# Two experts' weights side by side in one transfer, and the router's low parts on VectorE

## The chip, the cores and the metric

The kernel runs on one core of a Trainium2 chip. A core has TensorE (PE in the profile), VectorE (DVE), ScalarE (ACT), GpSimd (POOL), the queue engine SyncE (SP, which issues nearly all loads here), 16 DMA engines, and two on-chip memories: SBUF, 128 partitions wide, and PSUM, which TensorE writes. The metric is the device time of one execution in microseconds (us); lower is better.

## The reference, cut to what matters

The program is two dense transformer layers followed by two layers of a second kind. Each layer of the second kind is a sequence mixer, a layer norm, and a mixture of experts with 32 experts for 256 tokens of 1024 features. Only the mixture of experts is touched:

```python
def hierarchical_moe(x, w_rg, b_rg, w_re, b_re, w_gate, w_up, w_down):
    g_prob = softmax(xt @ w_rg + b_rg)                 # 4 groups
    g_w, g_idx = top_k(g_prob, 1)
    e_logits = (xt @ w_re + b_re).reshape(n_tok, 4, 8) # 8 experts in each group
    e_logits = take_along_axis(e_logits, g_idx)
    e_w, e_local = top_k(softmax(e_logits), 2)
    gate = g_w * e_w / sum(e_w)
    # each token goes through its two experts:
    h = silu(x @ w_gate[e]) * (x @ w_up[e])            # 1024 -> 512
    y += gate * (h @ w_down[e])                        # 512 -> 1024
# and around it: h = layer_norm(ALPHA * h + ffn)
```

An expert has three float32 matrices of 2 MB each (1 MB is 1,048,576 bytes here). All 32 experts of both layers are read, 192 MB a layer.

## The kernel before, in words

The function `moe` is called once for each of the two layers. It has three stretches.

**Loads.** The weights come in pieces of 1 MB, one piece for one half (`q`) of one matrix of one expert, 128 partitions of 8 KB. Their order is fixed in the list `order`: experts go in pairs, and stage by stage it holds gate and up of pair `st` and down of pair `st - 1`. They go through 20 places of 1 MB (`EW`): 3 in the tile `ew0`, 6 in `ew1`, 4 in `w` (the mixer's own weight ring), 5 in `hx` (the mixer's tile `hl`, where a piece is cut into two loads of 512 KB, 128 partitions of 4 KB), and one each in `x` and `xw`. `prefetch` (lines 1549 to 1559) issues loads on SP in that order; a load waits until TensorE has finished with what the place held before. The places come free at the end of the mixer one after another, the last two (`x`, `xw`) when the router has chosen.

**Router** (lines 1570 to 1664). For two tiles of 128 tokens: the normed rows `hc` on VectorE, 16 transposes and the logits on TensorE, then a chain of small VectorE instructions that finds the group and the two experts (`first_max`), ending in the choice matrix `M` (L1658). Three small matmuls on it give every token its place (`pos`, L1664). TensorE works in a mode whose operands are split into a high part `hH` (written by ScalarE, L1605) and a low part `hL = hc - hH` (written by GpSimd, L1606). The residual `ALPHA * h` is started in the accumulators by matmuls over `hH`, again `hH`, and `hL` (L1617).

**Experts** (lines 1752 to 1835). For every two pairs `gather` compares positions (`sel`, L1679) and multiplies `hH` and `hL` by the result (L1693), which gathers 64 tokens for each of 4 experts into `XG`. `first_products` (L1769) multiplies gate and up: the two experts of a pair fill the two halves of the array's columns, and the order of `steps` takes them in turn. Only in gate of the first pair are the steps sorted, all of one expert and then all of the other. `gated`, `turned`, `second_products` (L1797) and `combine` (L1809) follow. TensorE's order there is the order of the code (`manual_schedule`); elsewhere a scheduler sets it.

The two lines that the prediction speaks of most:

```python
for kk, i in sorted(steps, key=lambda s: s[1]) if (pr, nm) == (0, "gate") else steps:   # 1766
nc.gpsimd.tensor_tensor(hL[:, t], hc[:, t], hH[:, t].bitcast(F32), op=OP.subtract)       # 1606
```

Of the kernel before, what the change touches and what calls it, by code (L numbers as in the profile page):

```python
# [18 lines left out]
P = 128  # L19
S = 256  # L20
# [1475 lines left out]
EW = (("ew0", 3), ("ew1", 6), ("w", 4), ("hx", 5), ("x", 1), ("xw", 1))  # L1496
NX = sum(n for _, n in EW)


def moe(k, l, h, hsum, rows, const, cc):  # L1500
# [5 lines left out]

    names = [n for n, slots in EW for _ in range(slots)]
    for n, slots in EW:
        if n[:2] == "ew":
            k.rings[n] = (0, k.t(W, [P, slots, 2048], n))  # L1510
        elif n[0] == "x":
            k.rings.pop(n, None)
    k.rings["hx"] = (0, k.t(k.const, [P, 10, 1024], "hl", F32, 1))
    nsl, later = [0], []

    def wtile(src, ab, now):
        n = nsl[0]
        nsl[0] += 1
        ring = names[n % NX]
        if ring != "hx":  # L1520
            if ring not in k.rings:

                k.rings[ring] = (0, k.t(k.const, [P, 1, 2048], ring))
                k.late(k.rings[ring][1], anchor=M[:, 1, :1])
            w = k.slot(ring)
            wv = w.rearrange("p (a b) -> p a b", a=ab)
            if n < NX and ring[:2] == "ew":
                k.late(w, anchor=k.early)
            nc.sync.dma_start(wv[:, :now], src[:, :now])
            if now < ab:  # L1530
                later.append((wv[:, now:], src[:, now:]))
            return lambda i: wv[:, i]
        hs = []
        for q in range(2):
            w = k.slot("hx")
            wv = w.rearrange("p (a b) -> p a b", a=ab // 2)
            nc.sync.dma_start(wv, src[:, q * ab // 2:(q + 1) * ab // 2])
            hs.append(wv)
        return lambda i: hs[i // (ab // 2)][:, i % (ab // 2)]


    order = [((nm, q, e), a["moe_" + nm][l, e, q], 4)
             for st in range(NE // 2 + 1) for nm, pr in (("gate", st), ("up", st), ("down", st - 1))
             if 0 <= pr < NE // 2 for q in range(2) for e in (2 * pr, 2 * pr + 1)]
    index = {key: n for n, (key, _, _) in enumerate(order)}
    tiles = {}
    nxt = [0]

    def prefetch(n):
        while nxt[0] < min(n, len(order)):  # L1550
            key, src, ab = order[nxt[0]]
            tiles[key] = wtile(src, ab, ab // 2 if nxt[0] >= len(order) - 2 else ab)
            nxt[0] += 1
        if n >= len(order):

            while later:
                nc.sync.dma_start(*later.pop(0))
# [16 lines left out]
    for t in range(NT):  # L1574
# [3 lines left out]
        nc.vector.scalar_tensor_tensor(hc[:, t], h[:, t], mean, rows[0], op0=OP.add, op1=OP.mult)  # L1578
# [16 lines left out]
    nc.vector.tensor_tensor(boff, p, br, op=OP.add)  # L1595
    gl, el = k.t(W, [P, NT, 4], "rt"), k.t(W, [P, NT, NE], "rt2")
    for t in range(NT):
        for dst, cs in ((el, slice(4, 36)), (gl, slice(0, 4))):
            nc.vector.scalar_tensor_tensor(dst[:, t], plg[:, t, cs], ms[t][:, 2:3], boff[:, cs], op0=OP.mult, op1=OP.add)
    for t in range(NT):  # L1600
        for q in range(2):
            sl = slice(512 * q, 512 * q + 512)
            nc.vector.scalar_tensor_tensor(hc[:, t, sl], hc[:, t, sl], ms[t][:, 2:3], rows[1][:, sl],
                                           op0=OP.mult, op1=OP.add)
        nc.scalar.activation(hH[:, t], hc[:, t], AF.Copy)  # L1605
        nc.gpsimd.tensor_tensor(hL[:, t], hc[:, t], hH[:, t].bitcast(F32), op=OP.subtract)  # L1606
# [51 lines left out]
    nc.vector.tensor_tensor(v(M), v(M), og4, op=OP.mult)  # L1658
# [5 lines left out]
    nc.vector.scalar_tensor_tensor(pos, p, 1.0, M, op0=OP.add, op1=OP.mult)  # L1664
# [4 lines left out]
    slots = k.t(A, [P, 4, S], "slots", F32R)  # L1669

    def gather(pr, after=None):
# [42 lines left out]
    at = {}  # L1714
# [265 lines left out]
```

## Time and profile before

| | us |
|---|---|
| median of 3 timed runs | 1922.09 (1921.82 to 1927.83) |
| the profiled execution's own time | 1928.14 |
| its span in the profile | 1926.5 |
| mean granted TensorE clock, as a share of 2.4 GHz | 0.975 |

The page cuts the span into 40 slices. Two plateaus stand out in its row of gigabytes per second, slices 18 to 25 and 32 to 39: these are the two layers' expert stretches. TensorE is busy 94% of the span, but matmuls are pipelined and a busy TensorE may still be one that waits for its input, so the plateaus of the load row and the waits have to be read together.

### The profile page before, as it was taken

The page shows a single profiled execution, that of the slowest core. Times are in us where ns is not written, and L with a number is a line of the kernel's source. Part 1 is how long each engine was busy: PE and PEld are TensorE (multiplying, and loading weights), DVE is VectorE, ACT ScalarE, POOL GpSimd, SP SyncE. Part 2 cuts the span into 40 slices and gives each one's busy share as a digit, 9 for nine tenths or more (in the row PEclk, how much of TensorE's full clock was granted, in tenths as well). Part 3 has the DMA queues.
Part 4 walks back from the last instruction along what each step waited for, and adds up shares of the span by engine and source line. Part 5 has one row for each costly group of instructions (what it writes and reads, how often), then busy time and mean ns, then how long its engine had stood idle before and what let it go on. Part 6 is the DMA issues. An engine that isn't in the chain of part 4 may idle for free. (4 is left out here: it accounts for less than half of the span.)

```text
span 1926.5 us, 30281 instructions
## 1 busy us (share of the span) xinstructions
PE 1811.1 (94%) x12598; PEld 1231.2 (64%) x12598; DVE 770.3 (40%) x1491; ACT 595.2 (31%) x1022; POOL 134.7 (7%) x267
## 2 busy tenths in 40 slices
PE   8999999999998899999999999889999999999896
PEld 7889998989998788644444343377984444443333
DVE  5754545655456978411111011067782111111012
ACT  5554444554445644211111011144441111111011
POOL 1100000010010411100000000012120000000000
PEclk9999999999999999799999999998998999999998
DMA  6345554245563327799999999841488999999995
GB/s 250 109 153 196 177 204 154 88 146 183 194 224 132 112 89 312 264 414 418 418 418 418 418 418 418 358 168 46 143 332 328 413 418 418 418 418 418 418 418 206
DMA packets 90307, 541.65 MB, mean 281 GB/s; under 512 B 10416, under 2 KB 10928, under 8 KB 37936
## 3 DMA queue, kind: packets, MB, share of 16 engines
q1 hardware_dynamic: 87552, 531.21, 70.1%
q0 software_dynamic: 2320, 8.24, 1.4%
q8 instruction: 103, 1.69, 0.4%
q14 instruction: 44, 0.36, 0.1%
q10 hardware_dynamic: 288, 0.15, 0.0%
HBM read 538.52 MB, written 1.05 MB: 280 GB/s over the span
## 5 line engine op out<-in xcount | busy, mean ns | idle before, releaser
L161 DVE TENSOR_TENSOR hl<-w,hl 128x1024 fp32r<-128x1024 f32 (+2 forms) x252 | 295.6, 1182 | 224.3 <-ACT hl L159 218.2
L159 ACT ACTIVATE hl<-w 128x1024 fp32r<-128x1024 f32 (+2 forms) x252 | 256.4, 1026 | 282.2 <-PE aux L129 103.0
L1769 PE MATMUL aux<-ew_e,XG_e 128*64 128x512 f32 x992 | 253.9, 595 | 8.5 <-DMA ew_e<-in_moe_up 8.5
L1779 DVE SCALAR_TENSOR_TENSOR e_sh_e<-e_sh_e,e_kept_e,aux 128x512 f32<-128x512 f32 x32 | 23.9, 747 | 509.7 <-ACT e_sh_e L1778 497.0
L1769 PEld LDWEIGHTS aux<-ew_e,XG_e 128*64 128x64 f32 x992 | 82.2, 137 | 166.2 <-issue 148.1
L1788 ACT ACTIVATE e_sh_e<-m 128x512 f32<-128x512 f32 x32 | 19.1, 598 | 509.2 <-PE m L1786 509.2
L1769 PE MATMUL aux<-hl,XG_e 128*64 128x512 f32 x480 | 137.4, 604 | 10.1 <-DMA hl<-in_moe_up 6.1
L129 PE MATMUL aux<-hl_f,hl 128*128 128x256 f32 x1056 | 131.1, 283 | 0.6 <-DVE hl_f L245 0.3
L129 PEld LDWEIGHTS aux<-hl_f,hl 128*128 128x128 f32 x1056 | 129.3, 191 | 2.8 <-DVE hl_f L245 0.7
L1769 PE MATMUL aux<-w,XG_e 128*64 128x512 f32 x384 | 126.6, 594 | 4.5 <-DMA w<-in_moe_gate 4.5
L1801 DVE TENSOR_TENSOR e_y_e<-m,e_y_e 128x512 fp32r<-128x512 f32 x64 | 44.2, 691 | 215.0 <-ACT e_y_e L1800 215.0
L129 PE MATMUL m<-hl_f,hl 128*128 128x256 f32 x1056 | 129.7, 283 | 0.0
L129 PEld LDWEIGHTS m<-hl_f,hl 128*128 128x128 f32 x1056 | 127.7, 191 | 0.0
L182 PE MATMUL mm<-hl,m_f 128*128 128x512 f32 x528 | 123.4, 390 | 0.0
L1797 PE MATMUL m<-ew_e,e_sh_e 128*64 128x512 f32 x448 | 117.3, 602 | 0.0
L182 PEld LDWEIGHTS mm<-hl,m_f 128*128 128x128 f32 x528 | 97.8, 188 | 19.4
L1800 ACT ACTIVATE e_y_e<-m 128x512 fp32r<-128x512 f32 x64 | 38.2, 597 | 201.5 <-PE m L1797 201.5
L1769 PEld LDWEIGHTS aux<-hl,XG_e 128*64 128x64 f32 x480 | 41.8, 138 | 81.9 <-issue 51.6
L1693 PE MATMUL m<-e_y_e,e_h_e 128*128 128x256 f32 x256 | 69.2, 308 | 24.2 <-DVE e_y_e L1679 24.2
L1809 PE MATMUL mm<-e_y_e,slots_e 128*128 128x512 f32 x256 | 78.3, 429 | 6.1 <-PEq L1832 4.8
L1797 PE MATMUL m<-w,e_sh_e 128*64 128x512 f32 x240 | 81.5, 606 | 0.0
L1797 PEld LDWEIGHTS m<-ew_e,e_sh_e 128*64 128x64 f32 x448 | 35.6, 138 | 68.0 <-issue 63.6
(571 smaller groups left out, 2710.7 us busy)
## 6 DMA issues: line engine op xcount, KB each, us to landing
ew_e<-in_moe_gate SPq DMA_DIRECT2D x62, 1024.0 KB, 16.2
ew_e<-in_moe_up SPq DMA_DIRECT2D x62, 1024.0 KB, 17.4
ew_e<-in_moe_down SPq DMA_DIRECT2D x56, 1024.0 KB, 18.6
w<-in_w_gate_up SPq DMA_DIRECT2D x44, 1024.0 KB, 4.9
w<-in_w_in SPq DMA_DIRECT2D x36, 1024.0 KB, 5.0
hl<-in_moe_up SPq DMA_DIRECT2D x60, 512.0 KB, 11.4
hl<-in_moe_down SPq DMA_DIRECT2D x60, 512.0 KB, 13.2
hl<-in_moe_gate SPq DMA_DIRECT2D x60, 512.0 KB, 13.3
```

The lines of the kernel that those rows point to most:

```text
L129: self.nc.tensor.matmul(out, x, y, start=(i == 0 and j == 0), stop=(i == n - 1 and j == len(terms) - 1))
L159: nc.scalar.activation(vo(hv), s, AF.Copy)
L161: nc.vector.tensor_tensor(vo(lv), s, vo(hv).bitcast(F32), op=OP.subtract)
L182: self.nc.tensor.matmul(acc[t][h], u1, u2, start=(kg == 0 and q == 0), stop=(kg == n_k - 1 and q == len(terms) - 1))
L1693: nc.tensor.matmul(p[:, j], src[:, t, c], sel[t], start=n == 0, stop=n == 3)
L1769: nc.tensor.matmul(p[64 * i:64 * i + 64], xg[:, 4 * q + kk, o:o + CAP], tiles[nm, q, e](kk), start=(q == 0 and kk == 0), stop=(q == 1 and ...
L1779: i = nc.vector.scalar_tensor_tensor(s_, s_, at[pr][1], up, op0=OP.mult, op1=OP.mult)
L1788: nc.scalar.activation(hh, p, AF.Copy)
L1797: nc.tensor.matmul(p[64 * i:64 * i + 64], hh[:, f, 64 * i:64 * i + 64], tiles["down", hf, es[i]](f), start=f == 0, stop=f == 3)
L1800: nc.scalar.activation(yh, p, AF.Copy)
L1801: nc.vector.tensor_tensor(yl, p, yh.bitcast(F32), op=OP.subtract)
L1809: nc.tensor.matmul(acc[t][hf], sT[:, t * P:(t + 1) * P], ys[:, 2 * hf + q], start=False, stop=pr == last and q == 1)
```

## The change

What was two loads for two experts becomes one of 2 MB. The arrays in memory are laid out anew (`pack3`), so that the same partition's rows of both experts of a pair lie side by side: 16 KB in one run. The 20 places of 1 MB become 10 of 2 MB in the same tiles and of the same total. Two of the ten are made of two separate 1 MB places (`ew0` with `hx`, and `x` with `xw`) and still take two loads of 8 KB rows; the places in `hx` no longer take loads of 4 KB rows. The sorted order in the first gate is gone. The low parts `hL` are computed by VectorE, tile 0 after `M`, tile 1 after `sel`; their residual matmuls stand where the first, empty `combine` was, the gather takes both `hH` before both `hL`, and several router instructions get an `issue_after` that fixes their order. The small tile `al` lies in `slots` now.

```diff
-EW = (("ew0", 3), ("ew1", 6), ("w", 4), ("hx", 5), ("x", 1), ("xw", 1))
-NX = sum(n for _, n in EW)
+EW = (("ew0", 3), ("ew1", 6))
+NX, SPLIT = 10, 6
...
+    places = [("ew0", 0), ("ew1", 0), ("ew1", 2), ("ew1", 4), ("w", 2 * turn), ("w", 2 - 2 * turn),
+              (("ew0", 2), ("hx", 4)), ("hx", 0), ("hx", 2), (("x", 0), ("xw", 0))]
...
+    def fetch(n, parts=(0, 1)):
+        nm, q, pr = order[n]
+        src, at_ = a["moe_" + nm][l, pr, q], places[n % NX]
+        if type(at_[0]) is str:
+            t = part(*at_, 2)
+            if n < NX and at_[0][0] == "e":
+                k.late(t, anchor=k.early)
+            t = four(t)
+            now = 2 if n == len(order) - 1 else 4
+            nc.sync.dma_start(t[:, :, :now], src[:, :, :now])
...
+        for i in parts:
+            t = part(*at_[i], 1)
...
+            nc.sync.dma_start(t, src[:, i:i + 1])
...
-        nc.vector.scalar_tensor_tensor(hc[:, t], h[:, t], mean, rows[0], op0=OP.add, op1=OP.mult)
+        last = nc.vector.scalar_tensor_tensor(hc[:, t], h[:, t], mean, rows[0], op0=OP.add, op1=OP.mult).ins
...
-        nc.gpsimd.tensor_tensor(hL[:, t], hc[:, t], hH[:, t].bitcast(F32), op=OP.subtract)
...
+    def low_parts(t, after):
+        with tc.issue_after(after):
+            return nc.vector.tensor_tensor(hL[:, t], hc[:, t], hH[:, t].bitcast(F32), op=OP.subtract).ins
...
-    for src, i in ((hH, 0), (hH, 1), (hL, 0)):
+    def residual(src, i):
         for t in range(NT):
             for hf in range(2):
                 nc.tensor.matmul(acc[t][hf], al[:, i], src[:, t, hf * 512:(hf + 1) * 512],
                                  start=src is hH and i == 0, stop=False)
+    residual(hH, 0)
+    residual(hH, 1)
...
-    nc.vector.tensor_tensor(v(M), v(M), og4, op=OP.mult)
+    last = low_parts(0, nc.vector.tensor_tensor(v(M), v(M), og4, op=OP.mult).ins)
...
+        if pr == 0:
+            tail.append(low_parts(1, placed))
...
-                for t in range(NT):
-                    for src in (hH, hL):
+                for src in (hH, hL):
+                    for t in range(NT):
                         nc.tensor.matmul(p[:, j], src[:, t, c], sel[t], start=n == 0, stop=n == 3)
...
-                for kk, i in sorted(steps, key=lambda s: s[1]) if (pr, nm) == (0, "gate") else steps:
-                    e = es[i]
-                    o = (e % 4) * CAP
-                    nc.tensor.matmul(p[64 * i:64 * i + 64], xg[:, 4 * q + kk, o:o + CAP], tiles[nm, q, e](kk),
+                for kk, i in steps:
+                    o = (es[i] % 4) * CAP
+                    nc.tensor.matmul(p[64 * i:64 * i + 64], xg[:, 4 * q + kk, o:o + CAP], tiles[nm, q, pr](i, kk),
...
     def combine(pr, hf):
+        if pr == -1 and hf == 1:
+            residual(hL, 0)
...
-        o["moe_" + n] = i[f"moe_w_{n}_2"].reshape(L, NE, 2, 4, P, 512).swapaxes(3, 4)
+        o["moe_" + n] = i[f"moe_w_{n}_2"].reshape(L, NE // 2, 2, 2, 4, P, 512).transpose(0, 1, 3, 5, 2, 4, 6)
```

Three places show how the built programs differ. First SP, in the first of the two layers, from the mixer's last output weights on to the first loads that reuse a place. `128x2048` is a load of 1 MB, `128x1024` one of 512 KB, `128x4096` one of 2 MB. Before:

```order
L144 DMA w_67<-in_w_out 128x2048
L1529 DMA ew_e_704_7682<-in_moe_gate 128x2048 x2
L1529 DMA ew_e_705_7683<-in_moe_gate 128x2048
L1529 DMA ew_e_705_7683<-in_moe_up 128x2048 x4
L1529 DMA ew_e_705_7683<-in_moe_gate 128x2048
L1529 DMA w_67<-in_moe_gate 128x2048 x3
L1529 DMA w_67<-in_moe_up 128x2048
L1537 DMA hl_7684<-in_moe_up 128x1024 x6
L1537 DMA hl_7684<-in_moe_down 128x1024 x3
L1529 DMA x_7920<-in_moe_down 128x2048
L1537 DMA hl_7684<-in_moe_down 128x1024
L1529 DMA xw_7923<-in_moe_down 128x2048
```

And in the changed program:

```order
L144 DMA w_67<-in_w_out 128x2048
L1544 DMA ew_e_705_7683<-in_moe_gate 128x4096
L1544 DMA ew_e_705_7683<-in_moe_up 128x4096 x2
L1554 DMA ew_e_704_7682<-in_moe_up 128x2048
L1544 DMA w_67<-in_moe_gate 128x4096 x2
L1554 DMA hl_7684<-in_moe_up 128x2048
L1544 DMA hl_7684<-in_moe_up 128x4096
L1544 DMA hl_7684<-in_moe_down 128x4096
L1554 DMA x_7898<-in_moe_down 128x2048
L1554 DMA xw_7901<-in_moe_down 128x2048
```

The order of the bytes is the same; a load into `w` now needs two of the ring's four slots, and no `hl` load stands behind `x`. Second TensorE in the router, around the last logits (`aux`, with the transposed rows `hT`) and the residual matmuls (`mm_7814` and so on are accumulators, `e_h` and `e_l` are `hH` and `hL`). Before:

```order
L1584 MATMUL mm_7774<-const_69,XG_e_711_7725 128x128
L1617 MATMUL mm_7814<-e_h_e_709_7723,mw_e_729_7810 128x512
L1617 MATMUL mm_7815<-e_h_e_709_7723,mw_e_729_7810 128x512
L1617 MATMUL mm_7814<-e_h_e_709_7723,mw_e_729_7810 128x512
L1588 MATMUL aux_7728<-e_misc_e_707_7717,hT_e_724_7779 128x36 x4
L1617 MATMUL mm_7815<-e_h_e_709_7723,mw_e_729_7810 128x512
L1617 MATMUL mm_7814<-e_l_e_710_7724,mw_e_729_7810 128x512
L1617 MATMUL mm_7815<-e_l_e_710_7724,mw_e_729_7810 128x512
```

And in the changed program:

```order
L1593 MATMUL mm_7757<-const_69,XG_e_711_7708 128x128 x4
L1597 MATMUL aux_7711<-e_misc_e_707_7700,hT_e_722_7751 128x36 x4
L1597 MATMUL aux_7711<-e_misc_e_707_7700,hT_e_724_7762 128x36 x4
L1635 MATMUL mm_7795<-e_h_e_709_7706,slots_e_729_7791 128x512
L1635 MATMUL mm_7796<-e_h_e_709_7706,slots_e_729_7791 128x512
L1635 MATMUL mm_7795<-e_h_e_709_7706,slots_e_729_7791 128x512
```

No residual matmul stands ahead of the last logits any more, and none over `e_l` in the router. Third VectorE, from the choice `M` (the tile that L1658 and L1679 write) to the positions and `sel`. Before:

```order
L1658 TENSOR_TENSOR rt_e_739_7835<-rt_e_739_7835,rt_e_734_7830 128x64
L1728 SCALAR_TENSOR_TENSOR rt_e_755_7893<-rt_e_754_7892,rt_e_753_7891 128x2
L1729 RECIPROCAL rt_e_755_7893<-rt_e_755_7893 128x2
L1730 TENSOR_TENSOR rt_e_756_7894<-rt_e_755_7893,rt_e_754_7892 128x2
L1664 SCALAR_TENSOR_TENSOR e_kept_e_708_7718<-aux_7858,rt_e_739_7835 128x64
L1731 TENSOR_TENSOR rt_e_736_7832<-rt_e_736_7832,rt_e_755_7893 128x64
L1679 TENSOR_TENSOR e_y_e_746_7864<-const_69,e_kept_e_708_7718 128x256 x2
```

And in the changed program:

```order
L1679 TENSOR_TENSOR rt_e_739_7812<-rt_e_739_7812,rt_e_734_7807 128x64
L1621 TENSOR_TENSOR e_l_e_710_7707<-XG_e_711_7708,e_h_e_709_7706 128x1024
L1686 SCALAR_TENSOR_TENSOR e_kept_e_708_7701<-aux_7836,rt_e_739_7812 128x64
L1766 TENSOR_REDUCE s_e_757_7890<-aux_7887 128x1
L1700 TENSOR_TENSOR e_y_e_746_7842<-const_69,e_kept_e_708_7701 128x256 x2
L1621 TENSOR_TENSOR e_l_e_710_7707<-XG_e_711_7708,e_h_e_709_7706 128x1024
L1746 TENSOR_TENSOR rt_e_750_7867<-rt_e_727_7785,rt_e_735_7808 128x8
```

The two subtractions that write `e_l` stand on VectorE now, one between `M` and `pos`, one behind `sel`; the weights of the two experts (L1728 to L1734 before) come after them.

## Rows read from the trace of the kernel before

**Rows 1.** The page: the span, and GB/s in 40 equal slices.

```profile
span 1926.5 us, 30281 instructions
...
GB/s 250 109 153 196 177 204 154 88 146 183 194 224 132 112 89 312 264 414 418 418 418 418 418 418 418 358 168 46 143 332 328 413 418 418 418 418 418 418 418 206
```

**Rows 2.** Windows: stretch, length, busy (count) of PE to POOL, clock, DMA share, GB/s.

```profile
824.00:1222.00 398.00, 375.28 (x1812) 159.15 (x1809) 48.60 (x98) 45.63 (x84) 0.00 (x0) 0.99 1.02 418
...
1484.00:1880.00 396.00, 374.21 (x1810) 158.33 (x1808) 48.59 (x98) 45.64 (x84) 0.00 (x0) 0.99 1.02 418
...
890.00:901.00 11.00, 9.96 (x64) 6.58 (x66) 3.93 (x10) 2.56 (x5) 0.00 (x0) 1.00 1.02 409
904.00:940.00 36.00, 36.00 (x169) 12.86 (x166) 2.49 (x4) 2.28 (x4) 0.00 (x0) 1.00 1.01 420
```

**Rows 3.** Loads into `hl`: one row of SP's timeline, and the page's (median us to landing).

```profile
877.67 12.80 SPq L1537 DMA_DIRECT2D hl<-in_moe_down  x6
...
hl<-in_moe_down SPq DMA_DIRECT2D x60, 512.0 KB, 13.2
```

**Rows 4.** Timeline near the first layer's end, TensorE: start, us, engine, line, operation.

```profile
1224.59 3.65 PE L1769 MATMUL aux<-ew_e,XG_e 128*64 128x512 f32 x14 [1.31 <-DMA ew_e<-in_moe_up]
```

**Rows 5.** Windows in which the reuse of places begins, both layers.

```profile
802.00:824.00 22.00, 22.00 (x101) 8.96 (x99) 2.06 (x6) 3.13 (x5) 0.00 (x0) 1.00 0.80 294
...
1462.00:1484.00 22.00, 22.00 (x102) 9.09 (x102) 2.07 (x6) 3.13 (x5) 0.00 (x0) 1.00 0.87 327
```

**Rows 6.** Timeline of the first layer's router, all engines.

```profile
782.40 1.63 PE L1617 MATMUL mm<-e_h_e,mw_e 128*128 128x512 f32 x3
...
783.82 1.76 PE L1588 MATMUL aux<-e_misc_e,hT_e 128*128 128x36 f32 x8
...
785.62 0.67 DVE L1599 SCALAR_TENSOR_TENSOR rt_e<-aux,e_ms_e,e_boff_e 128x32 f32<-128x32 f32 x4
...
786.79 2.50 DVE L1637 SCALAR_TENSOR_TENSOR rt_e<-rt_e,const 128x8 f32<-128x8 f32 x2
...
786.84 2.36 POOL L1606 TENSOR_TENSOR e_l_e<-XG_e,e_h_e 128x1024 fp32r<-128x1024 f32 x1 [1.78 <-ACT e_h_e L1605]
...
791.65 0.22 DVE L1658 TENSOR_TENSOR rt_e<-rt_e,rt_e 128x64 f32<-128x64 f32 x1
...
793.46 0.23 DVE L1664 SCALAR_TENSOR_TENSOR e_kept_e<-aux,rt_e 128x64 f32<-128x64 f32 x1 [1.12 <-PE aux L1663]
...
794.85 0.58 PE L1693 MATMUL m<-e_y_e,e_h_e 128*128 128x256 f32 x1 [0.57 <-DVE e_y_e L1679]
```

**Rows 7.** The same in the second layer: two lines of `first_max`, the first product.

```profile
1446.08 0.34 DVE L1637 SCALAR_TENSOR_TENSOR rt_e<-rt_e,const 128x8 f32<-128x8 f32 x2
...
1446.59 2.21 DVE L1641 TENSOR_TENSOR rt_e<-const,rt_e 128x8 f32<-128x8 f32 x2
...
1457.57 5.95 PE L1769 MATMUL aux<-ew_e,XG_e 128*64 128x512 f32 x16
```

**Rows 8.** The page's costliest groups: VectorE's subtraction of the same shape.

```profile
L161 DVE TENSOR_TENSOR hl<-w,hl 128x1024 fp32r<-128x1024 f32 (+2 forms) x252 | 295.6, 1182 | 224.3 <-ACT hl L159 218.2
```

**Rows 9.** Timeline of the first products, and one later group of 16 in alternating order.

```profile
798.56 6.06 PE L1769 MATMUL aux<-ew_e,XG_e 128*64 128x512 f32 x16
...
802.88 9.55 SPq L1529 DMA_DIRECT2D ew_e<-in_moe_gate  x4
...
806.65 5.42 PE L1769 MATMUL aux<-ew_e,XG_e 128*64 128x512 f32 x16
```

**Rows 10.** Timeline: another 16 in alternating order, and a hole where `combine(-1, 1)` stands.

```profile
1219.62 3.65 PE L1769 MATMUL aux<-ew_e,XG_e 128*64 128x512 f32 x16 [1.32 <-DMA ew_e<-in_moe_up]
...
1495.59 0.36 PE L1693 MATMUL m<-e_y_e,e_h_e 128*128 128x256 f32 x1 [2.38 <-DVE e_y_e L1679]
```

**Rows 11.** Timeline between the layers: the mixer's weights, and VectorE's first use of one.

```profile
1256.07 4.20 SPq L144 DMA_DIRECT2D w<-in_w_in  x3
...
1266.90 1.22 DVE L161 TENSOR_TENSOR hl<-w,hl 128x1024 fp32r<-128x1024 f32 x1
```

More of the change, by code (lines that the diff above doesn't have):

```diff
@@ L1504, in moe @@
     iota, iotap = const["iota"], const["iotap"]
[L1507 to L1539, printed above, removed]
@@ L1542, in moe @@
[L1542 to L1545, printed above, removed]
-    tiles = {}
-    nxt = [0]
+    view = {n: k.t(W, [P, m, 2048], n) for n, m in EW}
+    view["hx"] = k.t(k.const, [P, 10, 1024], "hl", F32, 1).rearrange("p (a b) c -> p a (b c)", b=2)
+    n, t = k.rings["w"]
@@ new lines, in moe, with part, four @@
+    turn = n % 4 // 2
+    view["w"] = t
+    places = [("ew0", 0), ("ew1", 0), ("ew1", 2), ("ew1", 4), ("w", 2 * turn), ("w", 2 - 2 * turn),
+              (("ew0", 2), ("hx", 4)), ("hx", 0), ("hx", 2), (("x", 0), ("xw", 0))]
+    assert len(places) == NX
+    def part(n, o, m):
+        if n not in view:
+            view[n] = k.t(k.const, [P, 1, 2048], n)
+            k.late(view[n], anchor=M[:, 1, :1])
+        return view[n][:, o:o + m]
+    def four(t):
+        return t.rearrange("p e (a b) -> p e a b", a=4)
@@ new lines, in moe @@
+    order = [(nm, q, pr) for st in range(NE // 2 + 1) for nm, pr in (("gate", st), ("up", st), ("down", st - 1))
+             if 0 <= pr < NE // 2 for q in range(2)]
+    index = {key: n for n, key in enumerate(order)}
+    tiles = {}
+    nxt, later = [0], []
+    def fetch(n, parts=(0, 1)):
[8 more added lines that the diff above has]
+            nc.sync.dma_start(t[:, :, :now], src[:, :, :now])
+            if now < 4:
+                later.append((t[:, :, now:], src[:, :, now:]))
+            tiles[order[n]] = lambda i, kk: t[:, i, kk]
+            return
+        for i in parts:
+            t = part(*at_[i], 1)
+            if n < NX and at_[i][0][0] == "e":
+                k.late(t, anchor=k.early)
+            tiles[order[n] + (i,)] = t = four(t)
+            nc.sync.dma_start(t, src[:, i:i + 1])
+        tiles[order[n]] = lambda i, kk: tiles[order[n] + (i,)][:, 0, kk]
@@ L1595, in moe @@
     nc.vector.tensor_tensor(boff, p, br, op=OP.add)
+    for t in range(NT):
+        for q in range(2):
+            sl = slice(512 * q, 512 * q + 512)
+            with tc.issue_after(last):
+                i = nc.vector.scalar_tensor_tensor(hc[:, t, sl], hc[:, t, sl], ms[t][:, 2:3], rows[1][:, sl],
+                                                   op0=OP.mult, op1=OP.add)
+        nc.scalar.activation(hH[:, t], hc[:, t], AF.Copy)
     gl, el = k.t(W, [P, NT, 4], "rt"), k.t(W, [P, NT, NE], "rt2")
@@ L1663, in moe @@
     nc.tensor.matmul(p[:, 1], const["upper"], M[:, 1], start=False, stop=True)
[L1664 removed]
+    with tc.issue_after(last):
+        nc.vector.scalar_tensor_tensor(pos, p, 1.0, M, op0=OP.add, op1=OP.mult)
     sh = k.t(A, [P, 2, 512], "e_sh")
     ys = k.t(A, [P, 4, 512], "e_y", F32R)
[L1669 removed]
     def gather(pr, after=None):
```

52 lines of the change are left out of this document (27 added, 25 removed).

## The prediction

> **What bounds the kernel now.** I read the page first. In its row of GB/s two plateaus at 418 are the two expert stretches [rows 1], and the windows show that the 16 DMA engines have no gap there: a share of 1.02 at 418 GB/s over 398 us in the first layer and over 396 us in the second [rows 2]. TensorE is busy for 375.28 of the 398 us, so it has 22.7 us to spare over the stretch; toward its end it waits for loads, as in the row where the last gate-and-up weights of the first layer arrive 1.31 us after it wanted them [rows 4]. From that landing on TensorE sets the pace to the end of the layer. So the time of a layer is the moment at which the load stream becomes gapless, plus its bytes over its rate, plus a tail that the change leaves alone. Two things can move it: an earlier start of the gapless stream, and a higher rate.
>
> Where does the gapless stream start? Right after the first products, places come free too slowly: in the first 22 us of reuse the stream runs at 294 GB/s in the first layer and 327 in the second [rows 5]. Against 418 that is a loss of 22 × (1 − 294/418) = 6.5 us and 22 × (1 − 327/418) = 4.8 us. Before that the stream stands still until the first product has freed a place, so all that makes the first product late counts too.
>
> **The head: router and first gate.** The stream restarts when SP issues the first reuse, 802.88, that is 4.3 us after the first product begins at 798.56 [rows 9].
>
> What comes before 798.56? The last logits end at 783.82 + 1.76 = 785.58, and VectorE begins with them at 785.62 [rows 6]. Ahead of these logits TensorE does three residual matmuls, 1.63 us; the change moves them behind, but all transposes now come earlier and something of the time is the wait for ScalarE's copy. Between 0 and 1.63 I take 1.0. Next the choice takes until 791.87. In it a pair of tiny VectorE instructions takes 2.50 us while GpSimd's subtraction runs for 2.36 [rows 6]; the same pair took 0.34 in the second layer, where the next line of the chain met GpSimd's subtraction and took 2.21 [rows 7]. With the subtraction gone from GpSimd, 2.50 − 0.34 = 2.16 and 2.21 − 0.34 = 1.87 go.
>
> What is added: two subtractions on VectorE, 1.18 us each by the group of that shape [rows 8]. The first stands between the end of `M` (791.87) and `pos` (793.46), where VectorE waited for TensorE's small matmuls, the last 1.12 us of it for nothing else [rows 6]; the 1.6 us hold it. Uncovered it would cost 1.2. The second follows `sel`, as the gather does, and runs beside the gather's first six products, which do not need it. That costs between 0 and 1.2; I take 0.3, since most of it is covered. One reduction now ahead of `sel` costs 0.2. What these delay behind them, the expert weights in the small chain, is needed only after the first gate. So the first product comes 1.0 + 2.16 − 0.5 = 2.6 us earlier in the first layer and 1.0 + 1.87 − 0.5 = 2.3 in the second; I use 2.5 and 2.3.
>
> The first gate then runs in alternating order. Sixteen sorted records take 6.06 and 5.42 us [rows 9], sixteen alternating ones 3.65 [rows 10]; the first 16 sorted ones exceed the second by 0.6, which I take for a lower clock at their start and add here too. So the first 2 MB come free 4.2 us after the first product, about when 1 MB did before, and the stream restarts 2.5 (2.3) us earlier. Those 2 MB keep it busy for 5.0 us at 418 GB/s; the next 2 MB come free 2.1 us (half a gather) and 3.65 us later, 5.8 in all: a hole of 0.8 us. From there on a place comes free every 3.65 us or a little more and takes 5.0 to fill: no gap. With 1.0 us of start-up the loss is 1.8 us where it was 6.5 (4.8). The head gives 2.5 + 4.7 = 7.2 us and 2.3 + 3.0 = 5.3 us, 12.5 in both layers.
>
> The four residual matmuls over `hL` now stand in a hole of TensorE, where it waits 2.38 us for `sel` [rows 10]; four such matmuls are under 2.2 us (three took 1.63 at the slower clock, rows 6). Were the hole gone, they would eat into TensorE's 22.7 us to spare, not into the stream.
>
> **The rate.** Of every 20 MB, 5 go to `hl` in rows of 4 KB, the rest in rows of 8 KB. SP issued six `hl` loads from 877.67 to 890.47, and loads of this kind land 13 us later [rows 3]: they flow in the window 890 to 901, which runs at 409 GB/s, while 904 to 940, rows of 8 KB, runs at 420 [rows 2]. Per DMA engine (a sixteenth) a row of 4 KB takes 4096 / 25.56 = 160.2 ns and one of 8 KB 8192 / 26.25 = 312.1. The difference, 151.9 ns, is what 4 KB take; 8.3 ns are left as the fixed part. A row of 16 KB would then take 8.3 + 607.6 = 615.9 ns, which is 26.6 GB/s, or 425.6 for all 16. No row of the trace is that long, so this is an estimate; its bounds are 420 (what 8 KB do) and, below, any loss that long rows might bring (a rival). I take 425.6, since whether the fixed part belongs to the row or to the load, both halve.
>
> 20 MB are 20.97 million bytes: before, 15.73 at 420 and 5.24 at 409 make 50.3 us (417 GB/s, as the windows say). Now 16.78 at 425.6 and, for the four 1 MB places, 4.19 at 420 make 49.4. That is 0.88 us in every 20 MB. From the first reuse to the landing of the last gate-and-up weights there are 164 MB (pieces 20 to 183), 8.2 times as much: 7.2 us a layer, 14.4 in both. With all at 420 it would be 2.8 a layer.
>
> The Trainium skill, "DMA: Bandwidth & Descriptors", section "Where 436 GB/s comes from", speaks against this term: it says that for loads from HBM the HBM side binds, at about 358 GB/s a core. By that rule longer rows would change nothing, and the sum would be the head alone. The windows at 418 lie above that bound, so I give it little weight.
>
> **Costs at nothing.** SP's load into `w` waits for two slots of the ring instead of one; behind it stand only the loads into `hl` and `x`, which are wanted long after the first product. A piece lands whole, not by halves; TensorE alternates between both experts and needed both anyway. At the end of the first layer all four slots of `w` are taken, so that the next mixer's first weights are issued with the other three at 1256.07 and not earlier; VectorE first uses one at 1266.90 [rows 11], 10.8 us later, and a load of 1 MB takes 2.5 us of the stream. Without that cover it would cost some 3 us, once.
>
> **The sum.** 12.5 + 14.4 = 26.9 us. Off the profiled execution's 1928.14 that is 1901.2; that execution stands 6 us above the median of the timed runs, 1922.09, from which it gives 1895. TensorE keeps about 22.7 − 7.2 − 1 = 14 us to spare, so the loads still bound.
>
> **Rivals.** *Rows beyond 8 KB bring no more rate* (cut up on the way, or at a limit already). For it: no row of the trace is longer. Then 12.5 + 2 × 2.8 = 18.1 us: 1904. If the rate did not depend on the row's length at all, only the head would be left, 12.5 us: 1910; against that stands that rows of 4 KB and 8 KB differ, 409 to 420 [rows 2]. The rule of the Trainium skill cited above comes out there.
>
> *The head gives nothing*, because the second subtraction or the pairing of places holds the first reuse back as much as the rest gains. For it: the gather follows `sel` closely. Against: 2.1 us of the stall can hardly come back. Then 14.4 us: 1908.
>
> *Long rows slow the stream.* The place is the gapless stretch, 794 us in both layers: 16 engines each draw 16 KB in one run from addresses further apart. The price is 8 us for each percent. It decides against the change below 418 × 794 / (794 + 12.5) = 411.5 GB/s; at 400 it is 35.7 − 12.5 = 23 us slower: 1945. For it: the rate does depend on the load's form. Against: it rises with the row's length.
>
> **Chances.** Forecast 0.60 (1895, its own range 1888 to 1901); no more rate than 8 KB have 0.17; no gain in rate at all 0.03; no head 0.10; both together, about 1916, 0.05; long rows slower 0.05. The range 1885 to 1911 takes in these first four, and on its fast side an even lower fixed part or a head without the 0.5 and the hole. A measurement of this kernel can tell about 0.3%, 5.8 us, from no change: the three runs spread by that much. Faster by more: 0.92; within: 0.04; slower by more: 0.04.
>
> **What would show it.** In the changed profile: windows in mid-stretch at about 425 GB/s, lower only around the four 1 MB places; no GpSimd subtraction in the router, and no tiny VectorE instruction of 2 us there; the first product about 2.5 us earlier after the mixer's last output; the first two groups of 16 at about 4.2 and 3.65 us; over 400 GB/s in the windows right after the first reuse. The rate at 420 or less would make the largest term wrong; TensorE without waits for loads at the end of the stretch would show that it became the bound.

## The result: 1900.8 us, and the profile after

The changed kernel takes 1900.79 us, the median of five runs (1896.09 to 1917.61); the kernel before took 1925.99 in five runs beside it (1921.82 to 1928.54). The ratio is 0.988, 95% interval 0.984 to 0.991. That is 25.2 us less, against 26.9 forecast. It is faster by more than the measurement's bound, and the time lies in the range, 6 us above the predicted 1895.

The page of the changed kernel, its span and its row of GB/s in 40 slices; the plateaus of 418 in [rows 1] now stand at 426 to 427:

```profile
span 1915.9 us, 29809 instructions
...
GB/s 251 111 135 193 178 210 151 89 129 202 185 200 163 138 46 258 285 411 426 427 427 426 427 427 426 381 169 68 90 298 367 427 426 426 427 426 426 427 426 207
```

Windows of the changed kernel, columns as in [rows 2]: for each layer the 22 us from the first reuse on, and then the rest of the stretch:

```profile
811.50:833.50 22.00, 22.00 (x114) 9.08 (x116) 2.07 (x6) 3.03 (x5) 0.00 (x0) 1.00 0.94 363
833.50:1222.00 388.50, 365.24 (x1798) 153.95 (x1794) 48.61 (x98) 45.67 (x84) 0.00 (x0) 1.00 1.01 426
...
1460.80:1482.80 22.00, 22.00 (x114) 9.08 (x116) 2.07 (x6) 3.03 (x5) 0.00 (x0) 1.00 0.96 397
1482.80:1872.00 389.20, 365.71 (x1802) 154.45 (x1800) 48.62 (x98) 45.67 (x84) 0.00 (x0) 1.00 1.01 426
```

Against [rows 2] the rate rose from 418 to 426, and against [rows 5] the start from 294 and 327 to 363 and 397 (counted from the first reuse itself, before had 311 and 322, as its windows below show). TensorE is busy for 365 of 388.5 us, so it has 23 us to spare still; the stream bounds, as the end of the second layer says. A row of the timeline of TensorE there, which answers to [rows 4]:

```profile
1871.43 3.65 PE L1793 MATMUL aux<-ew_e,XG_e 128*64 128x512 f32 x16 [1.24 <-DMA ew_e<-in_moe_up]
```

Now the first layer's router and first gate, all engines, beside [rows 6, 9]:

```profile
785.83 1.97 PE L182 MATMUL mm<-hl,hl_m 128*128 128x512 f32 x8
...
793.52 1.41 DVE L1609 SCALAR_TENSOR_TENSOR XG_e<-XG_e,e_ms_e,row_e 128x512 f32<-128x512 f32 x2 [0.45 <-POOL e_ms_e L210]
...
793.79 1.98 PE L1597 MATMUL aux<-e_misc_e,hT_e 128*128 128x36 f32 x16 [0.25 <-ACT hT_e L1595]
...
796.39 0.28 DVE L1629 SCALAR_TENSOR_TENSOR slots_e<-const,slots_e 128x128 fp32r<-128x128 f32 x1
...
796.78 0.35 DVE L1656 TENSOR_TENSOR rt_e<-rt_e,rt_e 128x8 f32<-128x8 f32 x2
797.05 0.34 DVE L1658 SCALAR_TENSOR_TENSOR rt_e<-rt_e,const 128x8 f32<-128x8 f32 x2
...
799.74 0.23 DVE L1679 TENSOR_TENSOR rt_e<-rt_e,rt_e 128x64 f32<-128x64 f32 x1
799.88 1.22 DVE L1621 TENSOR_TENSOR e_l_e<-XG_e,e_h_e 128x1024 fp32r<-128x1024 f32 x1
...
801.02 0.22 DVE L1686 SCALAR_TENSOR_TENSOR e_kept_e<-aux,rt_e 128x64 f32<-128x64 f32 x1
...
802.03 0.63 PE L1717 MATMUL m<-e_y_e,e_h_e 128*128 128x256 f32 x3 [0.70 <-DVE e_y_e L1700]
802.14 1.22 DVE L1621 TENSOR_TENSOR e_l_e<-XG_e,e_h_e 128x1024 fp32r<-128x1024 f32 x1
...
803.41 0.58 PE L1717 MATMUL m<-e_y_e,e_l_e 128*128 128x256 f32 x1 [0.40 <-DVE e_l_e L1621]
...
805.84 5.58 PE L1793 MATMUL aux<-ew_e,XG_e 128*64 128x512 f32 x16
...
811.46 6.01 SPq L1544 DMA_DIRECT2D ew_e<-in_moe_gate  x2
...
813.46 3.65 PE L1793 MATMUL aux<-ew_e,XG_e 128*64 128x512 f32 x16
```

The pairs of tiny instructions that took 2.50 us (first layer) and 2.21 us (second layer) take 0.34 now (L1658 and L1662; only the first is shown), and from the end of the logits (795.77) to the end of `M` (799.97) pass 4.2 us where 6.3 and 6.1 passed. The windows of the kernel before, cut at the same events: the head of the first layer, and 22 us from the first reuse on in both layers:

```profile
772.50:802.90 30.40, 27.26 (x114) 21.28 (x114) 17.88 (x58) 7.10 (x13) 6.67 (x6) 0.61 0.68 252
802.90:824.90 22.00, 22.00 (x101) 8.95 (x100) 2.06 (x6) 3.13 (x5) 0.00 (x0) 1.00 0.84 311
...
1461.80:1483.80 22.00, 22.00 (x100) 8.96 (x100) 2.07 (x6) 3.13 (x5) 0.00 (x0) 1.00 0.86 322
```

In the changed kernel, the first subtraction stands between `M` and `pos`, and costs next to nothing; the second keeps the gather waiting for 0.40.

The span of this execution is only 10.6 us shorter than that of before, though each layer's expert stretch shrank by more. The place where it lost time is before the change's stretch, and a window there (columns as before) shows it:

```profile
668.00:697.00 29.00, 27.96 (x367) 20.43 (x367) 15.23 (x37) 8.53 (x27) 3.67 (x6) 0.53 0.01 2
```

The granted clock is at half (0.53) for 29 us of the first mixer; in the trace of before it was at 1.00 from 640 to 690. The changed kernel's run of 1917.61 is this execution. So neither span can be compared as a whole, and I cut each trace at four events that are found in all of them: the mixer's last matmul (the last group of L182, here 785.83 + 1.97 = 787.80), the first product, SP's first reuse, and the end of the last gate-and-up matmul. Each pair is first and second layer, in us:

| kernel | mixer's end to first product | to first reuse | to last gate-and-up | mid-stretch GB/s | median us |
|---|---|---|---|---|---|
| before | 26.1, 21.8 | 30.5, 26.0 | 455.8, 449.8 | 418 | 1925.99 |
| before_again | 22.4, 21.8 | 26.1, 26.1 | 449.7, 449.6 | 418 | (one run) |
| after | 18.0, 18.2 | 23.7, 23.0 | 437.9, 437.3 | 426 | 1900.79 |
| again | 18.0, 18.2 | 22.1, 22.3 | 436.9, 436.6 | 426 | 1900.02 |
| rows8 | 18.0, 18.2 | 23.7, 22.3 | 442.3, 441.7 | 421 | 1911.41 |
| rows4 | 18.0, 18.2 | 20.1, 20.5 | 448.1, 448.9 | 411, 412 | 1929.98 |
| parts_even2 | 18.0, 18.1 | 22.3, 21.7 | 439.2, 438.6 | 426 | 1900.19 |
| parts_even | 18.0, 18.1 | 25.3, 24.4 | 450.1, 449.4 | 426 | 1925.57 |
| gps_low | 21.9, 21.3 | 25.7, 25.0 | 440.8, 439.5 | 426 | 1910.74 |
| sorted_gate | 18.0, 18.2 | 25.4, 24.8 | 441.8, 441.1 | 426 | 1908.70 |
| before_alt | 22.5, 21.3 | 26.6, 25.6 | 448.7, 447.0 | 418 | 1920.29 |
| warm | 17.7, 19.4 | 21.4, 23.1 | 436.2, 437.6 | 426 | 1896.70 |
| warm5 | 18.5, 17.8 | 22.2, 21.5 | 436.5, 435.8 | 426 | 1896.45 |

### The profile page after: what moved, and what is told of

Read it like the earlier page. It is cut to its first block, busy times and chain, and to the rows that moved or that the text cites. A ratio compares the mean times of both kernels' runs of the same rounds, so it can differ in the third digit from the quotient of the medians.

```text
span 1915.9 us, 29809 instructions
## 1 busy us (share of the span) xinstructions
PE 1800.3 (94%) x12598; PEld 1227.4 (64%) x12598; DVE 771.4 (40%) x1495; ACT 594.7 (31%) x1022; POOL 126.1 (7%) x255
## 5 line engine op out<-in xcount | busy, mean ns | idle before, releaser
L1793 PE MATMUL aux<-ew_e,XG_e 128*64 128x512 f32 x992 | 243.5, 600 | 7.8 <-DMA ew_e<-in_moe_up 5.0
L1793 PEld LDWEIGHTS aux<-ew_e,XG_e 128*64 128x64 f32 x992 | 77.2, 139 | 164.5 <-issue 149.4
L1793 PE MATMUL aux<-hl,XG_e 128*64 128x512 f32 x480 | 127.7, 594 | 10.1 <-DVE e_y_e L1824 5.7
L182 PE MATMUL mm<-hl,m_f 128*128 128x512 f32 x528 | 123.5, 390 | 0.0
L1820 PE MATMUL m<-ew_e,e_sh_e 128*64 128x512 f32 x432 | 107.4, 596 | 3.5 <-DVE e_y_e L1824 2.8
L182 PEld LDWEIGHTS mm<-hl,m_f 128*128 128x128 f32 x528 | 97.9, 188 | 19.5
L1793 PE MATMUL aux<-w,XG_e 128*64 128x512 f32 x384 | 84.6, 593 | 2.8 <-DVE e_y_e L1824 2.8
L129 PE MATMUL aux<-hl_m,hl 128*128 128x256 f32 (+1 forms) x576 | 77.6, 291 | 1.7 <-ACT hl_m L782 0.8
L1717 PE MATMUL m<-e_y_e,e_h_e 128*128 128x256 f32 x256 | 56.5, 300 | 22.5 <-DVE e_y_e L1700 22.5
```

Of the source, the lines that this page charges most:

```text
L129: self.nc.tensor.matmul(out, x, y, start=(i == 0 and j == 0), stop=(i == n - 1 and j == len(terms) - 1))
L182: self.nc.tensor.matmul(acc[t][h], u1, u2, start=(kg == 0 and q == 0), stop=(kg == n_k - 1 and q == len(terms) - 1))
L1717: nc.tensor.matmul(p[:, j], src[:, t, c], sel[t], start=n == 0, stop=n == 3)
L1793: nc.tensor.matmul(p[64 * i:64 * i + 64], xg[:, 4 * q + kk, o:o + CAP], tiles[nm, q, pr](i, kk), start=(q == 0 and kk == 0), stop=(q == 1 ...
L1820: nc.tensor.matmul(p[64 * i:64 * i + 64], hh[:, f, 64 * i:64 * i + 64], tiles["down", hf, pr](i, f), start=f == 0, stop=f == 3)
```

## The experiments

Theory: about 7 us a layer come from the rate, by longer rows alone, and some 5 to 6 from the head, by the router without GpSimd's subtraction and by the alternating first gate. Rivals: another cause of the rate (a load's size, the number of loads), and a head that gives nothing.

**Both kernels a second time.** *again* is the changed kernel, no edit.

> The changed kernel once more, for its spread and for a second trace. Measured from the mixer's last matmul to the last gate-and-up matmul of the layer, the first trace gave 437.9 and 437.3 us (455.8 and 449.8 before the change); if these two figures are the change's and not that execution's, they come again within 2 us, the windows in mid-stretch show 426 GB/s, and the median lies between 1895 and 1905. If the half clock that its trace shows at 668 to 697 us was chance, it is absent here and the span is near 1898; if it belongs to the changed kernel, it is there again and the span is near 1914.

It took 1900.02 us (1896.27 to 1908.74), ratio to before 0.986 (0.983 to 0.989), span 1899.7. The stretch came again within 1 us in both layers, and the half clock did not (the granted clock is 0.94 from 640 to 700 us). Its first 22 us of reuse, both layers:

```profile
799.50:821.50 22.00, 22.00 (x114) 9.08 (x116) 2.07 (x6) 3.03 (x5) 0.00 (x0) 1.00 0.95 370
...
1444.50:1466.50 22.00, 22.00 (x114) 9.08 (x116) 2.07 (x6) 3.03 (x5) 0.00 (x0) 1.00 0.97 395
```

*before_again* is the kernel before, no edit.

> The kernel before, once more, for a second trace of its head. In the first trace the clock stood at half in the first layer's router from about 775 us on, and the first product came 26.1 us after the mixer's last matmul; in the second layer, with the half clock from about 1448, 21.8 us. If the long first one was this execution's, both layers come near 21.8 here and a layer's stretch near 450 us; if it belongs to the kernel, 26.1 and 455.8 come again.

Windows of it: from the mixer's end to the first reuse in the first layer, and the 22 us after the first reuse in both:

```profile
781.80:808.00 26.20, 21.83 (x116) 16.08 (x115) 17.73 (x58) 7.21 (x13) 6.75 (x6) 0.80 0.79 292
808.00:830.00 22.00, 22.00 (x100) 8.97 (x100) 2.07 (x6) 3.14 (x5) 0.00 (x0) 1.00 0.84 321
...
1465.60:1487.60 22.00, 22.00 (x100) 8.97 (x100) 2.06 (x6) 3.14 (x5) 0.00 (x0) 1.00 0.85 321
```

The first product came after 22.4 us and the stretch took 449.7: the granted clock of the head is 0.80, where it was 0.61 in the first trace. The 26.1 and 455.8 were that execution's. Typical stretches are thus 449.7 before and 437.2 after: 12.5 us a layer, 25.0 in both, which is the 25.2 of the medians. Nothing outside the two stretches is needed to explain the result.

**The row's length.** *rows8* (from the second fill of a place on):

```diff
-            nc.sync.dma_start(t[:, :, :now], src[:, :, :now])
+            for i in (range(2) if n >= NX else (slice(None),)):
+                i = slice(i, i + 1) if n >= NX else i
+                nc.sync.dma_start(t[:, i, :now], src[:, i, :now])
```

> Each 2 MB load is split by expert into two of 1 MB, so that a row is 8 KB again; all else stays. If the rate comes from the row's length (a fixed part of 8.3 ns per row), mid-stretch falls from 426 to 420 GB/s, a layer's stretch grows by 5 to 6 us, and the time by 10 to 12 us, to about 1912. If the rate has another cause (the stream's other order, the places), it stays at 426 and the time near 1901.

*rows4* cuts each of these once more along the row, `t[:, i, j:j + 2]`.

> Each 2 MB load is split into four of 512 KB with rows of 4 KB. By a fixed part per row, 160 ns for 4 KB: mid-stretch at 410 to 411 GB/s (two places in ten keep their 8 KB), 15 us more per layer, about 1930 in all, slower than before the change. By a limit that lies elsewhere (a rate of 426 whatever the row) 1901.

The windows of mid-stretch, first layer, of rows8 and of rows4:

```profile
832.80:1224.50 391.70, 367.79 (x1800) 156.86 (x1796) 48.63 (x98) 45.66 (x84) 0.00 (x0) 1.00 1.01 421
```

```profile
817.10:1218.10 401.00, 377.79 (x1806) 160.19 (x1804) 48.62 (x98) 45.64 (x84) 0.00 (x0) 0.99 1.02 411
```

rows8 has 421 GB/s, 4.8 us more a layer and 1911 us in all; rows4 has 411, 11 us more and 1930 (ratio to before 1.003, 1.001 to 1.006). The rates come within 1 GB/s and the totals within 1 us of those expected; the stretch of rows4 grew by 11 instead of 15 us. A quarter of a place is free before the whole, its first reuse came some 2.5 us earlier, and that pays back a part. Twice 11 us is less than the 29 us of the total; the rest lies outside the two stretches, and no run tells where.

To tell the row from the load's size, *parts64* keeps rows of 16 KB and halves the load by partitions, `t[i:i + 64]` with i = 0 and 64.

> Each 2 MB load is split by partitions into two of 1 MB of 64 rows each; rows stay at 16 KB. By the theory of the row's length 426 GB/s and a time near 1901 stay. By its rival, that the size of a load counts (a fixed part per load or per issue), it does as the split by expert does: 420 GB/s and 10 to 12 us more.

It took 2733.84 us, ratio 1.413 (1.407 to 1.419), which is neither theory's answer. A window of its first expert stretch:

```profile
1000.00:1300.00 300.00, 190.29 (x672) 73.25 (x672) 18.71 (x39) 17.28 (x32) 0.00 (x0) 0.81 1.01 222
```

All 16 engines are busy (1.01) at half the rate, so a row took twice as long. *parts_even* takes the same size of load from even and odd partitions, `t[i::2]`.

> Each 2 MB load is split into two of 1 MB that take the even and the odd partitions; rows stay at 16 KB. This asks again what the split at partition 64 was to ask. If the row's length sets the rate, mid-stretch shows 426 GB/s and a layer's stretch (mixer's last matmul to last gate-and-up matmul) 437 us, total near 1900. If a load's size or the number of loads sets it, 421 and 442 as in the split by expert, total near 1911. If the split at partition 64 was slow because any transfer of 64 partitions is slow, it comes out near 220 GB/s and 2730 again.

The rate is 426 GB/s:

```profile
816.20:1219.10 402.90, 370.16 (x1814) 155.25 (x1810) 48.60 (x98) 45.67 (x84) 0.00 (x0) 1.00 1.01 426
```

So it was the choice of partitions, not their number, and a load's size doesn't set the rate. But the total was 1925.57 and the stretch 450. SP's waits in its first layer's head (line, releaser, us in total, times, longest) show why:

```profile
SPq L1555 <- DVE e_kept_e L1761: 19.3, 1, 19.3
```

SP stood for 19.3 us in front of the first load into `hl`, issued at 794.25, 20.2 us after the mixer's end; in *again* that load went at 777.44, right at the mixer's end. 5 MB of the first fill came late by that much. Why that load came to wait for VectorE there, I did not find out. *parts_even2* leaves the first fill whole:

> As in the split by even and odd partitions, but the loads that fill the places for the first time stay whole, as they did in the split by expert. If the delay of 12 us there came from the first fill (the loads into the mixer's tile were issued 17 us late), and the row's length alone sets the rate: 426 GB/s, a layer's stretch of 437 us and a total near 1900. If twice as many loads cost anything by themselves: up to 442 and 1911.

It has 426 GB/s, stretches of 439.2 and 438.6 us, 1900.19 us (0.988, 0.986 to 0.991). A window of mid-stretch, first layer:

```profile
821.00:1210.80 389.80, 362.18 (x1792) 153.06 (x1790) 48.60 (x98) 45.63 (x84) 0.00 (x0) 1.00 1.01 426
```

With twice as many loads of half the size the total stays. Loads of 1 MB thus ran at 421 GB/s with rows of 8 KB (rows8) and at 426 with rows of 16 KB: the row's length is the cause of the rate. The stretch is 1.7 us longer, and I leave open by what.

**GpSimd again.** *gps_low*: `nc.vector` becomes `nc.gpsimd` in `low_parts`.

> The two low parts are computed by GpSimd again, at the place in the program where VectorE does them now. Theory: a GpSimd subtraction holds up small VectorE instructions beside it for some 2 us (2.50 and 2.21 instead of 0.34), and lasts 2.36 us instead of 1.2, so the first product comes 2 to 4 us later after the mixer's last matmul (18.1 us in the changed kernel), the layer's stretch grows from 437 to 439 to 441, and the total by 4 to 8 us to some 1905. Rival: the place alone, behind the choice, was what counted and the engine does not matter: 18.1, 437 and 1900 stay.

It took 1910.74 us (0.993, 0.991 to 0.996); the first product came 3.9 and 3.1 us later, and the stretch was 3.4 and 2.6 us longer. The expectation had its place wrong: `issue_after` did not hold GpSimd back. It took the work up at 781.69, as soon as ScalarE had written `hH`, beside the choice, where it had stood before. A few rows of its first router:

```profile
781.69 4.75 POOL L1621 TENSOR_TENSOR e_l_e<-XG_e,e_h_e 128x1024 fp32r<-128x1024 f32 x2 [1.76 <-ACT e_h_e L1611]
...
782.83 1.37 DVE L1629 SCALAR_TENSOR_TENSOR slots_e<-const,slots_e 128x128 fp32r<-128x128 f32 x1
...
784.32 2.29 DVE L1656 TENSOR_TENSOR rt_e<-rt_e,rt_e 128x8 f32<-128x8 f32 x2
...
789.51 0.64 PE L1682 MATMUL aux<-rt_e,const 128*128 128x32 f32 x2 [3.60 <-DVE rt_e L1679]
```

A tiny pair beside the subtraction takes 2.29 us where it took 0.35 (L1656), and another instruction 1.37 where it took 0.28 (L1629): two stalls of 1.95 and 1.1 make 3.05, just what the stretch of `M` lost (7.25 us against 4.2). So a GpSimd subtraction beside the choice brings the stall back. Whether GpSimd would stall anything if it ran behind the choice, where VectorE has the work now, no run shows: engine and place changed together.

**The order of the first gate.** *sorted_gate* puts `sorted(steps, key=lambda s: s[1])` back for the first gate.

> The first gate in the old order, one expert after the other; all else as changed. Theory: 16 such products take 5.4 us at full clock against 3.65, and with 2 MB places both experts' products must end before a place is free; so the first reuse comes 1.5 to 2 us later after the first product, the second place another 1.8, and the layer's stretch grows by 2 to 3.5 us, total by 4 to 7, to 1905. The prediction gave the whole of the order and the pairing 4.7 and 3.0 us. Rival: the stream makes it up and 437 and 1900 stay.

It took 1908.70 us (0.992, 0.989 to 0.995), and the stretch was 4.4 and 4.2 us longer: more than expected. The first products and the first reuse in the first layer:

```profile
804.80 7.35 PE L1793 MATMUL aux<-ew_e,XG_e 128*64 128x512 f32 x16
812.19 7.78 SPq L1544 DMA_DIRECT2D ew_e<-in_moe_gate  x2
814.18 5.42 PE L1793 MATMUL aux<-ew_e,XG_e 128*64 128x512 f32 x16
```

At half clock the 16 sorted ones take 7.35, and a 2 MB place waits for the last of them. *before_alt* is the converse: the kernel before, with `steps` in the first gate.

> The kernel before with one edit: its first gate in alternating order. Theory: the order is worth as much here as it cost in the changed kernel when put back (4.5 us a layer): 16 products take some 4 to 5 us at first and then 3.65 instead of 5.4, the windows after the first reuse rise from 311 and 322 GB/s, and the total falls by 4 to 9 us, to some 1920. Rival: with places of 1 MB the sorted order frees the first expert's place after 8 products, so the alternating order frees it later and nothing is gained: 1926.

It took 1920.29 us (0.997, 0.995 to 0.998), and the stretch was 1.0 and 2.6 us shorter than in before_again. A window of it, 22 us from the first reuse on:

```profile
802.70:824.70 22.00, 22.00 (x114) 9.08 (x116) 2.07 (x6) 3.13 (x5) 0.00 (x0) 1.00 0.94 364
```

With the sorted order this was 311 in the first trace and 321 in the second. The order helps either kernel, but the 1 MB places needed it less.

**A busy TensorE in the router.** *warm* fills the waits ahead of the positions and of the gather with matmuls that nobody reads:

```diff
+    def warm(n, after):
+        p = k.ps(tag="m3")
+        with tc.issue_after(after):
+            for j in range(n):
+                nc.tensor.matmul(p[:, (j % 4) * P:(j % 4 + 1) * P], k.ident, k.ident, start=True, stop=True)
...
-    residual(hH, 1)
+    warm(12, residual(hH, 1))
```

> In the changed kernel TensorE waits 1.63 us for the choice and 0.7 us for the positions, and just behind that the trace shows its clock at half for the gather (16 products in 3.8 us) and for part of the first gate (16 products in 4.0 to 5.6 us instead of 3.65). Here 12 and 4 small matmuls on a constant, whose result nobody reads, fill these two waits. If the idle engine is what brings the half clock, the gather takes about 2 us, the first product comes 1.5 to 2 us earlier after the mixer's last matmul (18.1 to about 16.3), the first 16 products take 3.65, the first reuse comes 2 to 3 us earlier and the layer's stretch falls from 437 to 434.5; total 4 to 5 us less, 1895. Rival: the clock falls for another reason, or the added matmuls hold up the choice: no earlier first product, 1900 or 1 to 2 us more.

It took 1896.70 us (0.986, 0.984 to 0.989). The first 16 products take 3.65 in both layers and the clock of the first layer's router is 1.00, as expected. But the first product comes 17.7 us after the mixer there, not 16.3, and in the second layer, where the granted clock still stands at 0.50 from 1423 to 1425, after 19.4 us:

```profile
1423.49 3.59 PE L1643 MATMUL m<-const 128*128 128x128 f32 x24
...
1426.91 0.31 PE L1689 MATMUL aux<-rt_e,const 128*128 128x32 f32 x2
```

The added ones run as 24, and the positions, whose input was ready at 1424.4, wait for them. *warm5* has 5 and 2.

> The added matmuls again, 5 and 2 instead of 12 and 4: the 12 went through TensorE as 24 passes in 3.6 us and held up the positions by 2.5 us in the second layer, while the wait that they fill is 1.6 us. If 5 (1.5 us) fit and still keep the clock up: first product 16 to 17 us after the mixer's last matmul (18.1 without them), first 16 products in 3.65, first reuse after 20 to 21 us (22 to 23.7 without), a layer's stretch of 435 to 436 us and a total of 1894 to 1898. If they are too few to keep the clock up: 18.1, a first group of 4 to 5.6, and 1900.

It took 1896.45 us (0.986, 0.984 to 0.988): the interval is that of *again*, so as a total this is no gain that can be told. The first 16 products take 3.67 and 3.65, but the first product comes after 18.5 and 17.8, not 16 to 17. The second layer's rows:

```profile
1425.14 0.69 PE L1643 MATMUL m<-const 128*128 128x128 f32 x4
...
1425.66 0.53 PE L1772 MATMUL aux<-rt_e,const 128*128 128x32 f32 x4
1426.23 0.19 DVE L1774 TENSOR_REDUCE s_e<-aux 128x1 f32<-128x32 f32 x1 [0.63 <-PE aux L1772]
```

The second group pushes back a matmul for which VectorE waits ahead of `sel`, and gives back a part of what the clock brings.

## Why the prediction was right, and where a term was off

- **What bounds, and the rate: right.** 426 GB/s against 425.6 forecast. With 164 MB (171.97 million bytes) the step from 418 to 426 is 411.4 − 403.7 = 7.7 us a layer, against 7.2. Taking out the fifth that stays at 8 KB, rows of 4, 8 and 16 KB take 160.2, 311.3 and 613.5 ns on one engine (409, 421 and 427 GB/s for 16). Each further 4 KB cost 151 ns, and 9 are left as the fixed part: the straight line that the prediction drew from two points holds at the third. By the rule of the Trainium skill that the prediction cited ("DMA: Bandwidth & Descriptors", "Where 436 GB/s comes from"), longer rows would have changed nothing; the runs do not agree, at 411, 421 and 426 on one core.
- **The stall: right, but a second one was overlooked.** 2.16 and 1.87 us forecast; against the trace that the prediction read, the choice became 2.1 and 1.9 shorter, and gps_low brought the stall back. In before_again the first layer's choice took 7.1 us, 2.9 more than after. Its rows show why: GpSimd's earlier subtraction, that of the other tile, held up VectorE too, in the last scaling of `hc`, so that VectorE began with the logits 1.15 us after they were ready at 790.83:

```profile
789.10 2.95 DVE L1603 SCALAR_TENSOR_TENSOR XG_e<-XG_e,e_ms_e,row_e 128x512 f32<-128x512 f32 x1 [1.60 <-PE mm L1584]
789.14 2.36 POOL L1606 TENSOR_TENSOR e_l_e<-XG_e,e_h_e 128x1024 fp32r<-128x1024 f32 x1 [2.55 <-issue]
789.75 1.08 PE L1588 MATMUL aux<-e_misc_e,hT_e 128*128 128x36 f32 x8
...
791.98 0.66 DVE L1599 SCALAR_TENSOR_TENSOR rt_e<-aux,e_ms_e,e_boff_e 128x32 f32<-128x32 f32 x4
```

That instruction takes some 0.7 us in the changed kernel (two in 1.41, L1609). In the first trace it took 2.83 and 1.94 us, but the logits were not ready sooner there, so it cost next to nothing.

- **The first product: too small.** 2.5 and 2.3 us forecast, 4.4 and 3.6 measured (22.4 in before_again to 18.0, 21.8 to 18.2; the first trace's 26.1 had 3.7 us of its own). In the first layer the logits gave 1.0, the choice 2.9 and the way from `M` to the first product 0.5. In the second layer the logits gave 0.9 (forecast 1.0) and the choice 1.9, but from `M` to the first product it became 0.8 shorter, not 0.5 longer: the way to `sel` became 1.0 shorter, as the small matmuls before `pos` ran at full clock (0.39 to 0.41 a pair; 0.61 to 0.64 before), and that from `sel` on 0.2 longer. The prediction had put nothing for the clock there.
- **The start of the reuse: too large, the step that failed.** The prediction took "the loss at reuse 1.8 us where it was 6.5 (4.8)". Its windows [rows 5] begin at 802.00 and 1462.00; the first began 0.9 us ahead of the first reuse, 802.88 [rows 9], so a wait was counted as loss that the earlier first product had already been credited with. From the reuse itself the loss before was 22 × (1 − 311/418) = 5.6 and, with 321 or 322 in three other stretches, 5.1. And 16 alternating products took 5.6, 4.8, 4.0 and 4.1 us, not 4.2, where the half clock reached into them (a granted clock of 0.50 from 804 to 808 us in the longest); the loss after was 3.3 and 1.5 (after), 2.9 and 1.6 (again). So 2.9 us a layer were gained there, in the mean, not 4.7 and 3.0.
- **The sum of a layer.** First reuse 3.3 us earlier after the mixer (26.1 to 22.8 in the mean), start 2.9, rate 7.7: 13.9, against 12.5 measured. Half a GB/s of rounding at each of the two rates, 0.5 us each, accounts for up to 1.0 of the 1.4; the rest stays open. The forecast had 2.4 for the first reuse, 3.9 for the start and 7.2 for the rate, in the mean of both layers. So the head came out right as a sum, 6.2 us, because the one term was 0.9 too small and the other 1.0 too large: that is luck. Put back singly, the parts cost 4.8 (rows8), 3.0 (gps_low) and 4.3 us (sorted_gate) of a layer's stretch; with some 2.9 for the rows of 4 KB (from 421 to 418 GB/s over 164 MB), which no run put back alone, that is more than 12.5, so they do not simply add.
- **TensorE's reserve.** 14 us forecast, 23 found. From the first reuse to the last gate-and-up matmul, 1923 recorded matmuls in each stretch kept TensorE busy for 399 to 401 us in both traces of before and for 391 in both after; the gate and up products account for all of that (232 to 234 us, then 222). In the first layer of before, 18 of their 64 groups of 16 took 3.8 us or more instead of 3.65, up to 6.2; after, 3 did. In rows8, where the two experts' loads are apart again, it is 16, in parts_even2 one. This fits groups that wait inside for the second expert's load, though no run shows that alone. So busy time held waiting, and the 22.7 us that it left were no measure of what TensorE could spare.
- **Costs at nothing: right as far as shown.** From one layer's last gate-and-up matmul to the next mixer's end, before_again and again both took 207.9 us: the next mixer's weights, issued later by the pairing, cost nothing that shows.
- **The time.** 26.9 forecast, 25.2 measured. The rest of the 6 us is the base: 1895 was counted from 1922.09, the median of three runs, and that of five is 1925.99.

## What to carry to other kernels

Where 16 DMA engines have no gap, look at the row's length first: two windows with different rows give a fixed part and a price per KB, and the next doubling can be read off the line. When places grow, check what must finish before one comes free; here the order of 16 matmuls was worth 4.3 us with 2 MB places and 1.8 with 1 MB. And compare traces between events that both contain, not by their spans: the changed kernel's stretch repeated within 1 us where its spans differed by 16. One trace is still not enough: the first layer of the kernel before gave 455.8 and then 449.7.

## What the runs showed of the hardware that was not expected

- **Which partitions a load covers.** Loads over partitions 0 to 63 and 64 to 127 ran at 222 GB/s, those over even and odd ones at 426, with the same rows and sizes. The Trainium skill, "SBUF — State Buffer", section "Door 1: The DMA port swizzle", says that partitions 0 to 63 reach only 8 of the 16 ports; the trace agrees, at 222 against 426. The page's next rule, that only a transfer over all 128 partitions reaches all ports (section "Can I just issue two DMAs to hit both halves?"), holds here for halves; loads of every second partition, each over 64 partitions only, ran at 426.
- **The clock outside the change.** In 13 traces (parts64 left out) the first mixer ended between 771.7 and 787.8 us, and the way from one stretch to the next mixer's end took 203.8 to 215.9, with the same work there. Where the two spans of the changed kernel differ by 16.2 us, the first mixer's end differs by 10.4 (787.8 and 777.4), the way between the stretches by 4.2 (212.1 and 207.9) and the two stretches together by 1.7.
